# Two places where side work is put into longer runs: the experts' gathers and scatters, and the second attention's products with values

## The chip, the cores and the metric

The kernel runs on one core of a Trainium2 chip. The metric is device time in microseconds (us), lower is better: the time of one execution on that core, as the median of several runs. One more execution was profiled; all rows below are from it. The engines are TensorE (PE, and PEld for its weight loads), VectorE (DVE), ScalarE (ACT), GpSimd (POOL) and SyncE (SP), which issues most of the DMAs.

## The reference

The input is one sequence of 512 tokens with 1024 features. Three blocks are chained: two transformer layers (attention, then a squared-ReLU MLP) and a third layer whose MLP is a mixture of experts. All is in float32. Two parts matter here.

The second layer's attention has 16 heads in 2 groups and three branches for each head, added with gates:

```
s_c = q . kc          # 31 compressed keys
o_c = softmax(s_c) . vc
o_s = softmax(masked q . k_sel) . v_sel      # selected blocks
o_w = softmax(masked q . k_win) . v_win      # window
out = g0 * o_c + g1 * o_s + g2 * o_w
```

With 512 tokens the number of kept blocks and the window both cover the whole sequence, so the second and the third branch are plain causal attention with their own keys and values.

The mixture of experts routes each of the 512 tokens to 2 of 32 experts; expert e computes

```
ys = (silu(xb @ w1[e]) * (xb @ w3[e])) @ w2[e]      # 1024 -> 512 -> 1024
out[token] += gate * ys
```

The weights of all experts are 32 x 3 x 1024 x 512 floats, 201 MB.

## The kernel before

The kernel runs the layers one after another; in time: first layer's attention, its MLP, second layer's attention, its MLP, third layer's attention, router and experts. The order of each engine's instructions is written out by hand: a function that is called issues its instructions there and then, and each engine works its own queue in order. Matrices of the dense layers are split in a high and a low part (`whi`, `wlo`), so that fp32r matmuls keep float32's accuracy.

**Second layer's attention** (`layer_1`). `pair_items(f)` (line 1350) makes the work for two heads, f from 0 to 7. It is a list of 10 items for a `Pipeline` (line 543). An item is one softmax over up to 512 columns (`softmax_item`, line 574): scores on PE (`qk`), maximum on DVE, exponential on ACT, scaling with the gate on POOL (line 606), transposes on PE (`T`, line 611), a copy of the transposed tile to SBUF (`hi`, line 614, into a tile of tag `PT`, 8 buffers), and products with the values on PE (`pv`, which calls `take`). The table `SM1` (line 28) says how many steps after the item's first step each part is issued: scores 0, maximum 1, exponential 2, scaling 3, transposes 5, copy 6, values 7, out 8. Each step of the pipeline issues the due parts of all items that are under way. The value products are done for two heads side by side by `two_columns` (line 624): each uses half of the columns of TensorE's array, with 64 columns of weights, which the profile prints as "128*64". Query blocks i of 128 rows are grouped as (3), (2 and 0), and (1). For (3) and for (2, 0) the branches b = 0 and 1 have items of their own, two (one for each head, a = 0 and 1), and `take` for a branch is called in the second of them: `both_pv` for the blocks of that branch. For block 1 both branches share two items. The first `take` also calls `started(f)`, the product with the compressed values (`pcT`), into the same PSUM bank. So there are five bursts of value products for each f.

**Experts** (`experts`, line 1905). Experts are taken in 16 pairs r, up to 64 tokens each. `first(r)` does the products with w1 and w3 (8 steps k), `second(r)` those with w2 (4 steps k). A step is one `product` (line 1989): it takes two weight tiles of 128 x 1024 floats, one of each expert of the pair, as the moving operand, and the two experts' tokens use the two halves of the array's columns ("128*64" again). Two instructions stand in the trace for each of its four float32 matmuls. The weight tiles stream through a ring of 24 SBUF tiles (`RING`, `load`); `two()` takes a pair of tiles and issues the loads of the pair 24 places further on, on SP's queue, which wait until the ring's tiles are free.

Beside the products, tokens must be brought to the experts and back by matmuls with one-hot matrices that use the whole array. `gather(q)` (line 1955) serves two pairs of experts, 34 units of work; `scatter([r-1, r])` (line 2052) adds the results of two pairs to x, 16 units of two matmuls each, a bank of four matmuls being added to x on DVE (line 2063). Both are generators in a list `work`; `fill(n)` (line 1935) issues the next n units. `FILL1` and `FILL2` (lines 82, 83) say after which step k of `first` and `second` how many units are issued: 16 in each `first`, in three places, 11 in each `second`, in two. `drain` issues what is left of one kind. `spread(r)` (line 2045) makes the one-hot matrix `ot` of the scatter with one matmul (32 rows of weights, "32*128") from `pick` and `posT` and a comparison on DVE; it stands inside `second`, after step 2. `turn(r)` transposes the hidden layer between the two products.

The loop (line 2084) goes `first(r)`, `second(r-1)`, `turn(r)`. Behind the last product, `second(15)`, what is left of the scatters is drained, and the output leaves block by block.

Of the kernel before, what the change touches and what calls it, by code (L numbers as in the profile page):

```python
# [9 lines left out]
F32 = mybir.dt.float32  # L10
F32R = mybir.dt.float32r
I32 = mybir.dt.int32
AF = mybir.ActivationFunctionType
# [5 lines left out]
S = 512  # L19
# [24 lines left out]
NE, CAP = 32, 64  # L44
# [34 lines left out]

FTILES = {'fraw': 8, 'fsum': 2, 'S2': 1, 'parth': 3, 'partl': 3, 'fwhi': 3, 'fwlo': 3}  # L80

FILL1 = {2: 5, 5: 5, 7: 6}
FILL2 = {1: 5, 3: 6}


@with_exitstack
def tile_kernel(ctx: ExitStack, tc: tile.TileContext, I, out, stage=None, start=None):
    nc = tc.nc
# [10 lines left out]
    def ps(rows=128, cols=512):  # L99
        t = psum.tile([128, 512], F32, tag="ps", name="ps")  # L100
        return t[:rows, :cols]
# [17 lines left out]
    ident = cst[:, K_ID:K_ID + 128]  # L119
# [504 lines left out]
    def two_columns(o, at, of, start=False, stop=False):  # L624

        for c in range(2):
            nc.tensor.matmul(o[c * 64:c * 64 + 64, at], *of(c), start=start, stop=stop, skip_group_check=True,  # L627
                             tile_position=(0, c * 64))
# [6 lines left out]
    def lazy(f):  # L635
        box = []

        def get():
            if not box:
                box.append(f())  # L640
            return box[0]
        return get
# [439 lines left out]
    def layer_1():  # L1082
# [244 lines left out]
        def started(f):  # L1327
            o = ps()
            two_columns(o, slice(0, S), lambda a: (vcs[f // 4][:, f % 2 * 2 + a], pcT[:, f // 2, :]), start=True)
            return o  # L1330

        def ended(f, o):
            nc.scalar.activation(oh[:, f], o, AF.Copy)
            nc.vector.tensor_tensor(ol[:, f], o, oh[:, f], ALU.subtract)
# [9 lines left out]
        def both_pv(i, at, b, p, o, g):  # L1344

            for j in range(i + 1):
                two_columns(o, slice(i * 128, i * 128 + 128),
                          lambda c: (vsw[:, j, b * 2 + g], p[c]()[:, at + j * 128:at + j * 128 + 128]), stop=j == i)

        def pair_items(f):  # L1350
            o = lazy(lambda: started(f))
            new = lambda: att.tile([128, S], F32, tag="PT", name="PT", bufs=8)
            out = []
            nothing = lambda: None

            def items(segs, take, use=nothing):
                p = [lazy(new), lazy(new)]
                for a in range(2):
                    out.append(softmax_item(SM1, segs(a), qk, lambda n, i: cmask[:, 384 - i * 128:],
                                            lambda n, i: gate[:, i, n // 2 * 3 + 1 + n % 2:n // 2 * 3 + 2 + n % 2],  # L1360
                                            p[a], (lambda: take(p)) if a else nothing, use if a else nothing, a))
            for part in ((3,), (2, 0)):
                for b in range(2):
                    def take(p, part=part, b=b):
                        for i, at in zip(part, (0, 384)):
                            both_pv(i, at, b, p, o(), f // 4)
                    items(lambda a, b=b, part=part: [(4 * f + 2 * a + b, i) for i in part], take)

            def last(p):
                for b in range(2):  # L1370
                    both_pv(1, 256 * b, b, p, o(), f // 4)
            items(lambda a: [(4 * f + 2 * a, 1), (4 * f + 2 * a + 1, 1)], last, lambda: ended(f, o()))
            return out

        items = [cmp_item(0, 0), cmp_item(0, 2)]
        for f in range(8):
            if f == 3:
                items += [cmp_item(1, 0), cmp_item(1, 2)]
            items += pair_items(f)
# [380 lines left out]


    def moe():
        posT = att.tile([NE, S], F32R, name="posT")
        ghl = att.tile([128, NT, NE, 2], F32R, name="ghl")
        with phase("experts") as sub:
            experts(sub, posT, ghl)
        with phase("overflow") as sub:
            overflow(sub)
# [136 lines left out]
    def experts(sub, posT, ghl):  # L1905
# [3 lines left out]
        work, picks, ot = [], [], {}  # L1909
        pairs = NE // 2  # L1910
        last = pairs - 1
# [17 lines left out]
        def two():  # L1929
            i = used[0]  # L1930
            used[0] += 2
            load(i + len(RING))
            return tiles[i:i + 2]

        def fill(n):
            while n and work:
                if next(work[0], work) is work:
                    work.pop(0)
                else:
                    n -= 1  # L1940

        def drain(name):
            while any(w.__name__ == name for w in work):
                fill(1)
# [44 lines left out]
        def product(p, k, nk, xs, w):  # L1989

            for n in range(2):
                for b in range(2):
                    nc.tensor.matmul(p[n][half(b)], xs[:, half(b)], w[b][:, n * 512:n * 512 + 512],  # L1993
                                     start=k == 0, stop=k == nk - 1)

        def first(r):
            p = ps(), ps()
            for k in range(KD):
                product(p, k, KD, xt[r // 2][k][:, r % 2 * 128:r % 2 * 128 + 128], two())
                if k == KD - 1:  # L2000
                    s = sub.tile([128, S], F32, tag="silu", name="silu", bufs=1)
                    hs[r] = sub.tile([128, S], F32, tag="hs", name="hs", bufs=2)
                    nc.scalar.activation(s, p[0], AF.Silu)  # L2003
                    nc.vector.scalar_tensor_tensor(hs[r], s, gcol[r], p[1], ALU.mult, ALU.mult)
                fill(FILL1.get(k, 0))

        def turn(r):
            p = ps()
# [6 lines left out]
        def second(r):  # L2015
            if r % 2 == 0:
                drain("scatter")
            h = hid.pop(r)
            p = ps(), ps()
            ys[r] = [sub.tile([128, D], F32R, tag="y" + s, name="y" + s, bufs=2) for s in "hl"]  # L2020
            for k in range(4):
                product(p, k, 4, h[:, k], two())
                if k == 3:
                    for n in range(2):
                        nn = slice(n * 512, n * 512 + 512)
                        split_evac(ys[r][0][:, nn], ys[r][1][:, nn], p[n])
                if k == 2:
                    spread(r)
                if r < last:
                    fill(FILL2.get(k, 0))  # L2030
            if r >= last - 1:
                work.append(scatter([r]))
            elif r % 2:
                work.append(scatter([r - 1, r]))
            if r == last:
                drain("scatter")

        def picking(r):

            pick = sub.tile([NE, 128], F32R, tag="pick", name="pick", bufs=2)  # L2040
            nc.gpsimd.tensor_copy(pick.rearrange("p (e s) -> p e s", e=2),  # L2041
                                  ident[0:NE, 2 * r:2 * r + 2][:, :, None].to_broadcast([NE, 2, CAP]))
            picks.append(pick)

        def spread(r):

            p = ps()
            nc.tensor.matmul(p, picks[r], posT, start=True, stop=True)  # L2048
            ot[r] = sub.tile([128, S], F32R, tag="ot", name="ot", bufs=3)
            nc.vector.tensor_scalar(ot[r], p, iota[:, 64:65], None, op0=ALU.is_equal)  # L2050

        def scatter(rs):

            for t in range(NT):
                for n in range(2):
                    p = ps()
                    nn = slice(n * 512, n * 512 + 512)
                    for j, r in enumerate(rs):
                        for a in range(2):
                            nc.tensor.matmul(p, ot[r][:, t * 128:(t + 1) * 128], ys[r][a][:, nn],  # L2060
                                             start=j == 0 and a == 0, stop=j == len(rs) - 1 and a == 1)
                        yield
                    nc.vector.tensor_tensor(x[:, t, nn], p, x[:, t, nn], ALU.add)
                if rs[-1] == last:
                    finish(t)
# [1 line left out]

        make_o(0)
        sub.tile([128, S], F32R, tag="ot", name="ot", bufs=3)
        sub.tile([NE, 128], F32R, tag="pick", name="pick", bufs=2)  # L2070
        sub.tile([128, 8], F32, tag="gs", name="gs", bufs=2)
        sub.tile([128, PAD], F32, name="pad")
        for c in "ab":
# [1 line left out]
        load(len(RING))  # L2075
        nc.scalar.activation(ghl[:, :, :, 0], gates, AF.Copy)
        nc.gpsimd.tensor_tensor(ghl[:, :, :, 1], gates, ghl[:, :, :, 0], ALU.subtract)
        p = ps(NE)
        for t in range(NT):
            nc.tensor.transpose(p[:, t * 128:(t + 1) * 128], posm[:, t], ident)  # L2080
        nc.scalar.activation(posT, p, AF.Copy)
        work.append(gather(0))
        drain("gather")
        for r in range(pairs + 1):
# [211 lines left out]
```

## Time and profile before

| | |
|---|---|
| runs before, us | 2154.09, 2155.61, 2158.60 (median 2155.61) |
| the profiled execution, us | 2152.04 |
| its span, first to last instruction, us | 2150.2 |
| TensorE busy, share of the span | 2064.6 us, 96% |
| VectorE, ScalarE, GpSimd busy | 52%, 37%, 20% |
| moved from HBM | 324.49 MB |
| second layer's attention, steady part | about 784 to 917 us |
| experts' products | 1650 to 2129 us |

Times of rows are microseconds from the span's start. Matmuls are pipelined, so one matmul's duration is longer than the step from its start to the next one's; steps are what count. Weight loads (PEld) run ahead of the matmuls where they can.

### The profile page before, as it was taken

How to read it: one execution, taken by the hardware profiler on the slowest of the kernel's cores; microseconds unless marked ns; L12 is line 12 of the kernel's file. 1: busy time of each engine (PE TensorE's matmuls, PEld its weight loads, DVE VectorE, ACT ScalarE, POOL GpSimd, SP SyncE). 2: the span in 40 equal slices, each digit the busy share in tenths (PEclk: the TensorE clock that was granted, in tenths of full speed). 3: DMA queues.
4: the chain of work that ended last, by engine and by line, in shares of the span. 5: the costliest groups of instructions: out<-in, count | busy, mean ns of one | idle time of the engine just before them, and what ended most of it. 6: DMA issues, size and time to landing. Idle time of an engine off the chain costs nothing.

```text
span 2150.2 us, 28736 instructions
## 1 busy us (share of the span) xinstructions
PE 2064.6 (96%) x10871; PEld 1503.5 (70%) x10871; DVE 1111.4 (52%) x2273; ACT 798.0 (37%) x1530; POOL 421.8 (20%) x548
## 2 busy tenths in 40 slices
PE   7999999999999999999999999989998999999997
PEld 6786688888888777888888887767766444444443
DVE  5486544768764567634768766443724132222223
ACT  4525533434443357733434444453632101010000
POOL 2344420000002355620000002553352000000000
PEclk9999999999999999999999999999998999999998
DMA  4231025233232210024242231302045999999994
GB/s 136 70 98 30 21 89 166 72 125 108 69 94 90 61 39 2 2 89 138 75 143 85 89 98 58 108 20 88 11 162 209 418 417 408 409 416 403 406 405 185
DMA packets 118829, 328.58 MB, mean 153 GB/s; under 512 B 10604, under 2 KB 12716, under 8 KB 118688
## 3 DMA queue, kind: packets, MB, share of 16 engines
q1 hardware_dynamic: 115888, 318.87, 40.9%
q0 software_dynamic: 2800, 7.84, 1.2%
q8 instruction: 87, 1.43, 0.3%
q14 instruction: 54, 0.44, 0.1%
HBM read 324.49 MB, written 2.11 MB: 152 GB/s over the span
## 4 chain that ended last, share of the span: by engine, by line
PE 57%; DVE 4%; ACT 2%; POOL 1%; issue 1%; DMA 0%; DVEq 0%; POOLq 0%; ACTq 0%
PE ps L1993 16%; PE ps L404 10%; PE ps L347 8%; PE ps L696 5%; PE ps L1964 3%; PE ps L2060 2%; PE ps L627 2%; PE ps L611 2%; PE ps L1341 2%; POOL wlo L280 1%; PE ps L1710 0%; ACT P L1598 0%; PE ps L2011 0%; DVE room L469 0%; PE ps L1712 0%
## 5 line engine op out<-in xcount | busy, mean ns | idle before, releaser
L267 ACT ACTIVATE whi<-raw 128x1024 fp32r<-128x1024 f32 (+2 forms) x162 | 168.4, 1042 | 384.4 <-PE ps L404 155.0
L280 POOL TENSOR_TENSOR wlo<-raw,whi 128x512 fp32r<-128x512 f32 (+1 forms) x132 | 168.8, 1301 | 381.4 <-ACT whi L267 368.3
L282 DVE TENSOR_TENSOR wlo<-raw,whi 128x1024 fp32r<-128x1024 f32 (+2 forms) x96 | 118.3, 1233 | 225.1 <-ACT whi L267 224.9
L1993 PE MATMUL ps<-ew,xt 128*64 128x512 f32 x1024 | 229.9, 597 | 0.0
L404 PE MATMUL ps<-oTl,whi 128*128 128x512 f32 (+2 forms) x576 | 211.4, 371 | 1.4 <-DVE oTl L311 1.4
L404 PE MATMUL ps<-oTh,whi 128*128 128x512 f32 (+2 forms) x576 | 211.6, 371 | 0.5 <-ACT oTh L310 0.5
L404 PE MATMUL ps<-oTh,wlo 128*128 128x512 f32 (+2 forms) x576 | 166.7, 370 | 0.0
L1993 PEld LDWEIGHTS ps<-ew,xt 128*64 128x64 f32 x1024 | 69.4, 137 | 128.2 <-issue 111.3
L347 PE MATMUL ps<-whi,uTh 128*128 128x512 f32 (+2 forms) x384 | 151.3, 395 | 2.3 <-ACT uTh L310 2.3
L347 PE MATMUL ps<-whi,uTl 128*128 128x512 f32 (+2 forms) x384 | 147.7, 386 | 2.3 <-DVE uTl L311 2.2
L404 PEld LDWEIGHTS ps<-oTl,whi 128*128 128x128 f32 x576 | 108.5, 188 | 20.9 <-DVE oTl L311 2.1
L404 PEld LDWEIGHTS ps<-oTh,whi 128*128 128x128 f32 x576 | 108.5, 188 | 19.6 <-ACT oTh L310 1.0
L347 PE MATMUL ps<-wlo,uTh 128*128 128x512 f32 (+2 forms) x384 | 117.5, 386 | 4.2 <-POOL wlo L280 4.2
L1993 PE MATMUL ps<-ew,hid 128*64 128x512 f32 x512 | 118.4, 600 | 0.7 <-ACT hid L2013 0.7
L404 PEld LDWEIGHTS ps<-oTh,wlo 128*128 128x128 f32 x576 | 104.8, 188 | 18.7
L647 DVE TENSOR_TENSOR x<-ps,x 128x512 f32<-128x512 f32 x124 | 82.0, 684 | 65.0 <-PE ps L347 38.0
L598 ACT ACTIVATE P<-P,nm 128x384 f32<-128x384 f32 (+2 forms) x192 | 106.3, 557 | 22.3 <-DVE nm L591 19.1
L445 POOL DMA_DIRECT2D room<-gains x5 | 2.8, 566 | 566.3 <-DVE fwlo L289 566.3
L591 DVE CUSTOM_DVE_ANT_0 P<-ps,cst 128x128 f32<-128x128 f32 (+3 forms) x168 | 74.9, 473 | 37.9 <-POOL P L606 18.6
L2041 POOL CAST pick<-cst 32x128 fp32r<-32x128 f32 x16 | 4.9, 307 | 443.5 <-PE ps L2048 443.5
L2003 ACT ACTIVATE silu<-ps 128x512 f32<-128x512 f32 x16 | 9.6, 597 | 212.8 <-PE ps L1993 212.8
L347 PEld LDWEIGHTS ps<-wlo,uTh 128*128 128x128 f32 x384 | 72.5, 192 | 20.3 <-POOL wlo L280 6.9
(548 smaller groups left out, 4544.7 us busy)
## 6 DMA issues: line engine op xcount, KB each, us to landing
ew<-w SPq DMA_DIRECT2D x384, 512.0 KB, 9.4
raw<-mlp_w SPq DMA_DIRECT2D x80, 512.0 KB, 3.7
fraw<-mlp_w SPq DMA_DIRECT2D x48, 512.0 KB, 5.8
raw<-w_in SPq DMA_DIRECT2D x24, 512.0 KB, 3.8
raw<-ab_w_in SPq DMA_DIRECT2D x20, 512.0 KB, 3.6
raw<-c_w_in SPq DMA_DIRECT2D x12, 512.0 KB, 3.6
raw<-ab_w_out SPq DMA_DIRECT2D x8, 512.0 KB, 3.9
raw<-c_w_out SPq DMA_DIRECT2D x8, 512.0 KB, 3.7
```

Of the source, the lines that this page charges most:

```text
L267: nc.scalar.activation(hi[:, :w], raw[:, :w], AF.Copy)
L280: nc.gpsimd.tensor_tensor(lo[:, h], raws[r][:, h], hi[:, h], ALU.subtract)
L282: nc.vector.tensor_tensor(lo[:, :w], raws[r][:, :w], hi[:, :w], ALU.subtract)
L347: nc.tensor.matmul(p, a[:, tt], w[:, k], start=u == 0 and n == 0, stop=u == nk - 2 and n == 5)
L404: nc.tensor.matmul(p[:, tt], w[:, k, ff], b[:, u + k, tt], start=start and n == 0, stop=u == nk - 2 and n == 5, **kw)
L591: nc.vector.tensor_tensor_reduce(st["p"][:, a], st["s"][c], in1(h, i), 1.0, 3e38, ALU.add, ALU.min, st["nm"][:, c:c + 1])
L598: nc.scalar.activation(p, p, AF.Exp, scale=-1.0, bias=st["nm"][:, c:c + 1], accum_out=st["sm"][:, c:c + 1])
L611: nc.tensor.transpose(st["t"][:, j:j + 128], st["p"][:, j:j + 128], ident)
L647: nc.vector.tensor_tensor(xs, p, xs, ALU.add)
L696: nc.tensor.matmul(acc[b][t], p[:, 2 * h + k, tt], v[:, k], start=begins and h == 0 and m == 0, stop=m == 5, skip_group_check=True)
L1964: nc.tensor.matmul(v, htok[a][:, t, c * 128:(c + 1) * 128], oo[q][:, t], start=t == 0 and a == 0, stop=t == NT - 1 and a == 1)
L1993: nc.tensor.matmul(p[n][half(b)], xs[:, half(b)], w[b][:, n * 512:n * 512 + 512], start=k == 0, stop=k == nk - 1)
```

## The change

In the second layer's attention the items of both branches keep their order, but `take` is called once for a group of blocks, in the last of its four items, and does `both_pv` for both branches. In the experts, `fill` is called once at the end of `first` (16 units) and once at the end of `second` (11 units), and `spread` moves from after step 2 to the end of `second`. `pick` and `posT` get 128 partitions instead of 32, with zeros in the new ones. The last two pairs' scatters become one, like the others.

```diff
-FILL1 = {2: 5, 5: 5, 7: 6}
-FILL2 = {1: 5, 3: 6}
+FILL1, FILL2 = 16, 11
...
-            def items(segs, take, use=nothing):
-                p = [lazy(new), lazy(new)]
+            def items(segs, p, take, use=nothing):
                 for a in range(2):
                     out.append(softmax_item(SM1, segs(a), qk, lambda n, i: cmask[:, 384 - i * 128:],
                                             lambda n, i: gate[:, i, n // 2 * 3 + 1 + n % 2:n // 2 * 3 + 2 + n % 2],
-                                            p[a], (lambda: take(p)) if a else nothing, use if a else nothing, a))
+                                            p[a], take if a else nothing, use if a else nothing, a))
             for part in ((3,), (2, 0)):
+                p = [[lazy(new), lazy(new)] for _ in range(2)]
+
+                def take(p=p, part=part):
+                    for i, at in zip(part, (0, 384)):
+                        for b in range(2):
+                            both_pv(i, at, b, p[b], o(), f // 4)
                 for b in range(2):
-                    def take(p, part=part, b=b):
-                        for i, at in zip(part, (0, 384)):
-                            both_pv(i, at, b, p, o(), f // 4)
-                    items(lambda a, b=b, part=part: [(4 * f + 2 * a + b, i) for i in part], take)
+                    items(lambda a, b=b, part=part: [(4 * f + 2 * a + b, i) for i in part], p[b], take if b else nothing)
...
-        posT = att.tile([NE, S], F32R, name="posT")
+        posT = att.tile([128, S], F32R, name="posT")
...
                     nc.vector.scalar_tensor_tensor(hs[r], s, gcol[r], p[1], ALU.mult, ALU.mult)
-                fill(FILL1.get(k, 0))
+            fill(FILL1)
...
-                if k == 2:
-                    spread(r)
-                if r < last:
-                    fill(FILL2.get(k, 0))
-            if r >= last - 1:
-                work.append(scatter([r]))
-            elif r % 2:
+            spread(r)
+            if r < last:
+                fill(FILL2)
+            if r % 2:
                 work.append(scatter([r - 1, r]))
...
-            pick = sub.tile([NE, 128], F32R, tag="pick", name="pick", bufs=2)
+            pick = sub.tile([128, 128], F32R, tag="pick", name="pick", bufs=2)
...
+        nc.gpsimd.memset(posT.bitcast(F32), 0.0)
...
-        nc.scalar.activation(posT, p, AF.Copy)
+        nc.scalar.activation(posT[0:NE], p, AF.Copy)
```

## Rows read from the trace of the kernel before

**Rows 1.** Stretches: us, busy of PE, PEld, DVE, ACT, POOL, clock, DMA.

```profile
1650.00:2129.00 479.00, 478.31 (x2346) 214.29 (x2345) 111.08 (x224) 46.78 (x79) 3.97 (x14) 1.00 0.98 395
1700.00:1750.00 50.00, 50.00 (x255) 24.45 (x252) 10.48 (x29) 4.18 (x7) 0.28 (x1) 1.00 1.03 418
1850.00:1900.00 50.00, 50.00 (x242) 22.40 (x241) 11.90 (x25) 4.13 (x7) 0.28 (x1) 1.00 1.01 406
```

**Rows 2.** Waits, 1650 to 2128: us, times, longest; weight loads only.

```profile
PEld ps L1964 <- issue: 34.1, 42, 0.8
...
PEld ps L2048 <- issue: 13.0, 16, 0.8
...
PEld ps L2011 <- issue: 7.3, 9, 0.8
PEld ps L1977 <- issue: 5.7, 7, 0.8
PEld ps L2060 <- ACT silu L2003: 4.9, 6, 0.8
PEld ps L2060 <- issue: 2.4, 3, 0.8
```

**Rows 3.** Timeline of PE: start, us, line, tiles, form, count.

```profile
2068.49 13.95 PE L1993 MATMUL ps<-ew,xt 128*64 128x512 f32 x64
2082.27 5.32 PE L1993 MATMUL ps<-ew,hid 128*64 128x512 f32 x24
...
2087.95 1.94 PE L1993 MATMUL ps<-ew,hid 128*64 128x512 f32 x8
...
2098.20 5.37 PE L1993 MATMUL ps<-ew,xt 128*64 128x512 f32 x24
...
2103.84 0.40 PE L2060 MATMUL ps<-yl,ot 128*128 128x512 f32 x1
...
2105.70 0.40 PE L2060 MATMUL ps<-yl,ot 128*128 128x512 f32 x1
2106.03 3.65 PE L1993 MATMUL ps<-ew,xt 128*64 128x512 f32 x16
```

**Rows 4.** Waits of SP's DMA queue, 1700 to 1750 us.

```profile
SPq L1927 <- DMA ew<-w: 33.9, 39, 1.5
```

**Rows 5.** Waits of SP's DMA queue, 1850 to 1900 us.

```profile
SPq L1927 <- PE ps L1993: 28.3, 19, 6.6
```

**Rows 6.** Tile ew, all 384 loads: issue to landing.

```profile
DMA to landing us min/median/max: 3.4/9.4/10.6
```

**Rows 7.** Timeline of SP's queue from 1650 us.

```profile
1652.06 47.52 SPq L1927 DMA_DIRECT2D ew<-w  x42
```

**Rows 8.** Timeline of DVE from 2129 us.

```profile
2130.46 9.65 DVE L2063 TENSOR_TENSOR x<-ps,x 128x512 f32<-128x512 f32 x16
```

**Rows 9.** Groups of instructions from 1560 us: count, busy us, mean ns, idle before.

```profile
L2050 DVE TENSOR_SCALAR ot<-ps,cst 128x512 fp32r<-128x512 f32 x16 | 12.0, 751 | 93.2 <-PE ps L2048 93.2
```

**Rows 10.** Timeline of PE in the second attention's steady part.

```profile
865.23 0.48 PE L1341 MATMUL ps<-kst01h,qst 128*128 128x512 f32 x1
...
865.78 0.60 PE L611 MATMUL ps<-cst,P 128*128 128x128 f32 x4
866.14 0.48 PE L1341 MATMUL ps<-kst11h,qst 128*128 128x512 f32 x1
...
866.78 1.09 PE L627 MATMUL ps<-PT,vsw 128*64 128x128 f32 x16
```

**Rows 11.** Timeline at the start of the second attention's pipeline.

```profile
781.90 1.97 PE L627 MATMUL ps<-PT,vsw 128*64 128x128 f32 x14 [3.62 <-DVE PT L614]
782.03 4.30 POOL L606 TENSOR_SCALAR P<-P,sm,gate 128x384 f32<-128x384 f32 x8 [2.35 <-DVE sm L603]
```

**Rows 12.** Stretches of the second attention; columns as in Rows 1.

```profile
780.00:800.00 20.00, 18.10 (x156) 15.68 (x157) 14.51 (x57) 14.66 (x46) 10.39 (x18) 0.83 0.08 28
...
850.00:870.00 20.00, 20.00 (x195) 16.55 (x195) 14.35 (x58) 15.48 (x47) 11.87 (x20) 1.00 0.01 2
```

More of the change, by code (lines that the diff above doesn't have):

```diff
@@ L1360, in items, with last @@
                                             lambda n, i: gate[:, i, n // 2 * 3 + 1 + n % 2:n // 2 * 3 + 2 + n % 2],
-                                            p[a], (lambda: take(p)) if a else nothing, use if a else nothing, a))
+                                            p[a], take if a else nothing, use if a else nothing, a))
             for part in ((3,), (2, 0)):
-                for b in range(2):
-                    def take(p, part=part, b=b):
-                        for i, at in zip(part, (0, 384)):
-                            both_pv(i, at, b, p, o(), f // 4)
-                    items(lambda a, b=b, part=part: [(4 * f + 2 * a + b, i) for i in part], take)
-            def last(p):
+                p = [[lazy(new), lazy(new)] for _ in range(2)]
[3 more added lines that the diff above has]
+                            both_pv(i, at, b, p[b], o(), f // 4)
+                for b in range(2):
+                    items(lambda a, b=b, part=part: [(4 * f + 2 * a + b, i) for i in part], p[b], take if b else nothing)
+            p = [lazy(new), lazy(new)]
+            def last(p=p):
                 for b in range(2):
                     both_pv(1, 256 * b, b, p, o(), f // 4)
-            items(lambda a: [(4 * f + 2 * a, 1), (4 * f + 2 * a + 1, 1)], last, lambda: ended(f, o()))
+            items(lambda a: [(4 * f + 2 * a, 1), (4 * f + 2 * a + 1, 1)], p, last, lambda: ended(f, o()))
             return out
@@ L2038, in picking @@
         def picking(r):
-            pick = sub.tile([NE, 128], F32R, tag="pick", name="pick", bufs=2)
+            pick = sub.tile([128, 128], F32R, tag="pick", name="pick", bufs=2)
             nc.gpsimd.tensor_copy(pick.rearrange("p (e s) -> p e s", e=2),
-                                  ident[0:NE, 2 * r:2 * r + 2][:, :, None].to_broadcast([NE, 2, CAP]))
+                                  ident[:, 2 * r:2 * r + 2][:, :, None].to_broadcast([128, 2, CAP]))
             picks.append(pick)
@@ L2069, in experts @@
         sub.tile([128, S], F32R, tag="ot", name="ot", bufs=3)
-        sub.tile([NE, 128], F32R, tag="pick", name="pick", bufs=2)
+        sub.tile([128, 128], F32R, tag="pick", name="pick", bufs=2)
         sub.tile([128, 8], F32, tag="gs", name="gs", bufs=2)
```

## The prediction

> **What bounds the kernel now.** The profiled execution took 2152.0 us around a span of 2150.2 us; the median of the runs is 2155.6 us, 3.6 us more. I read first the busy times by stretch. From 1650 to 2129 us, the experts' stage, TensorE is busy 478.3 of 479 us, and the core's DMA engines show a share of 0.98, over 1 in the stretches inside it [rows 1]: two resources are full together, and a gain on one is limited by the other. So two clocks must be kept.
>
> TensorE's clock: in the stage it never waits for a result. What it loses stands in the waits of the weight loads. Each time a run of the experts' products (64 columns of weights, "128*64") is left for another kind of matmul, the next weight load comes some 0.8 us late instead of being prefetched: 42 + 16 + 9 + 7 + 6 + 3 = 83 times [rows 2]. The price of one such departure and return is read from the timeline [rows 3]. Eight products without a break took 2082.27 - 2068.49 = 13.78 us, 1.72 each. Three products and 10 scatter matmuls took 2106.03 - 2098.20 = 7.83 us; the scatter's own step is (2105.70 - 2103.84)/8 = 0.23 us, so 7.83 - 3 x 1.72 - 10 x 0.23 = 0.36. For three products with one `spread` between them: 2087.95 - 2082.27 - 5.17 - 0.23 = 0.28. I take 0.33.
>
> The stream's clock: 384 tiles of 0.524 MB go through a ring of 24. Where SyncE waits only for earlier transfers (33.9 of 50 us) [rows 4] the stream makes 418 GB/s, 1.254 us a tile; where it waits mostly for TensorE to free a tile (28.3 of 50 us) [rows 5] it makes 406 [rows 1]. So the stream is at its own limit in some stretches, and held back only a little in others.
>
> **Experts, TensorE alone.** `fill(16)` after `first` and `spread` + `fill(11)` + `turn` after `second` leave 2 departures per pair of experts. Pair 14 has nothing to fill after `first`, and pair 15's `spread` joins the scatter behind the last product, so inside the products 15 + 15 = 30 remain of 83. Saved: 53 x 0.33 = 17.5 us, and 0.2 for the `spread` that leaves: 17.7. No matmul is added. The longer runs are covered: 16 units of scatter are eight banks of four matmuls, 0.92 us a bank, against an addition of 0.60 us each [rows 8], so VectorE keeps up.
>
> **Experts, the stream.** The stretch most exposed is pair 14 and the first product of pair 15, where no fill is left between the products: TensorE asks for 24 tiles in 12 x 1.72 = 20.6 us, the stream needs 30. Where does each stand at the last product of `first(15)`? Before, it started at 2106.03 + 1.72 = 2107.75 [rows 3]. By then 79 of the 83 departures lie behind it before and 28 after: 51 x 0.33 = 16.8 us earlier; and the 20 scatter matmuls that stood in front of it now stand behind it: 4.6 more. TensorE would be there at 2086.3. That product needs the 368th tile. The first 24 are loaded early; the 25th is issued at 1652.06 [rows 7], unchanged, as it waits for the first product, and lands 3.4 us later at best [rows 6], at 1655.5. 343 more tiles at 418 GB/s end at 1655.5 + 430.2 = 2085.7: no wait. At the 406 of the other stretch (1.291 us) they end at 2098.3: a wait of 12. With TensorE freeing tiles earlier, SyncE should wait for transfers nearly always, so I lean to 418, but slower spots that belong to the stream itself will stay: I take 413 GB/s, 1.270 us, 2090.9, a wait of 4.6. Behind that point come 16 units of scatter (7.4 us) in which the stream gets ahead again, and the last 16 tiles don't bind. Sum: -17.7 + 4.6 = -13.1 us (bounds -17.7 and -5.7).
>
> The Trainium skill bears on this end: DMA: Bandwidth & Descriptors (section Bandwidth) gives 425 GB/s as measured for one core alone on a large load, and 358 as a core's share of HBM. By 425 TensorE would never wait and the stage would give the whole 17.7 (rival A); by 358 this stage could not exist, since 201 MB would take 562 us. The trace's 418 agrees with the first figure and contradicts the second here.
>
> **Experts, edges.** Before, pair 14's scatter ran while the last results were evacuated, and 16 additions ended at 2130.46 + 9.65 = 2140.1 [rows 8]. Now pair 15's `spread` is compared on VectorE (0.75 us [rows 9]) behind those evacuations: ready at 2130.46 + 0.75 = 2131.2 on the same time axis. The first two scatter matmuls go before it, TensorE then waits some 1.5 us, 30 matmuls at 0.23 end about 2138.1, the last one's tail and an addition make it 2139.2: -0.9 (bounds +1 and -1.5), as eight additions instead of 16 no longer set the pace. The memory set of `posT` on GpSimd delays ScalarE's copy of it, which is first needed behind the second pair's `first`; queued behind it on ScalarE is only the gather's evacuation. `pick` grows only in partitions. Nothing (bounds 0 and +0.5).
>
> **Second layer's attention.** In its steady part TensorE also runs without a gap, 20.00 of 20 us [rows 12]. From a step's scores to its values it is 866.78 - 866.14 = 0.64 us, from scores to the next transposes, without values, 865.78 - 865.23 = 0.55 [rows 10]: the entry alone costs 0.09. With the return a burst of values costs between that and the 0.33 above; I take 0.28, near the price that holds both ways. Bursts per pair of heads go from 5 to 3, over 8 pairs 16 fewer: -4.5 us (bounds -5.3 and -1.4). Against it: at the start of the pipeline TensorE stands 3.6 us for the first values' copy [rows 11], and meanwhile, and at a lowered clock, does the first burst (14 matmuls in 1.97 us). Now that burst moves two steps back, TensorE stands at the transposes instead, which wait for GpSimd's scaling starting at 782.03 [rows 11], and the opening product with the compressed values and both bursts come after the stall: I charge +2 (bounds 0 and +4). Longer bursts in one step and none in three could let ScalarE fall behind; it is busy 15.48 of 20 us there [rows 12] and no row shows TensorE late on it: nothing, but +2 as an upper bound. Value tiles live two steps longer, 4 or 5 of 8 buffers: no wait. Sum -2.5 (bounds -5 and +4).
>
> **Sum.** -13.1 - 0.9 - 2.5 = -16.5: 2135.5 in the profiled execution's terms, 2155.6 - 16.5 = 2139.1 against the median. Forecast 2139 us.
>
> **Rivals.**
> A, the stream keeps pace: at 418 GB/s or better TensorE never waits: -17.7 - 0.9 - 2.5 = -21.1, or -23 if the attention gains all: 2134. For it: the 418 in undisturbed stretches. Against: even there TensorE's pace of consumption was lower than it will be, and the margin at the critical product is 0.6 us.
> B, the stream falls back: long runs without a product (23 units, over 9 us, every second pair) free no tile; if the ring fills, transfers stop and restart, and the mean falls to 406: -5.7 - 0.9 - 2.5 = -9.1, 2146.5; at 400, 1.311 us a tile, the wait is 18.8 and the stage gains nothing: with the rest -2.3, 2153, no change.
> C, slower: TensorE's clock. Granted 1.00 throughout the stage [rows 1], it fell to a mean of 0.83 in the 20 us around the attention's 3.6 us stall [rows 12], between the 1.2 and 2.4 GHz levels. If TensorE, waiting for tiles in pairs 14 and 15, drops to 1.2 GHz, a product takes 3.44 us instead of the stream's 2.54: 20 products x 0.9 = 18 us, and the gain is gone (about 2157); if the lower level lasts to the last product, 8 x 1.72 + 7.4 = 21 more, 2178. [...] Against it: TensorE stays two thirds busy.
> D, it doesn't do what it says: the cost sits in each return to products with fresh weights, not in the change of kind, or `spread` at 128 rows costs what it saves: no change, 2153 to 2156.
>
> **How the numbers follow.** Forecast (the stream catches TensorE in pair 14) 0.55; A 0.2; B 0.15, a fifth of it within no change; C 0.05; D 0.05. The range takes A and most of B: 2131 to 2150. A measurement of this kernel tells about 0.2%, 4.3 us, from no change. Faster by more: 0.55 + 0.2 + 0.12 + a little = 0.88; same 0.07; slower 0.05.
>
> **What would show it.** Departures from products fall from 83 to about 30, each at the same price. A run of 12 products between two bursts should appear; TensorE's waits on weight tiles first show in pair 14 or 15, and DMA there reads 413 to 418 GB/s. If no wait on tiles shows and the last product ends 17 us earlier, A is right. If GB/s stays at 406 with waits from pair 8 on, B. The granted clock below 1.00 before the tail would show C. In the attention, three value bursts per pair of heads instead of five, and a longer first stall. A stage of products that is not at least 8 us shorter makes the account of the departures wrong.

## The result, and the profile after

The changed kernel takes 2139.69 us (median of 4 runs, 2138.48 to 2140.22) against 2156.52 us of the kernel before in the same runs: a ratio of 0.9922, 95% interval 0.9904 to 0.9939. The forecast was 2139. Its profiled execution took 2139.59 us around a span of 2137.8, which is 12.4 us less than the span before, while the medians differ by 16.8. So the two profiles are compared stage by stage, not by their ends. Line numbers of the changed kernel are one less or two more than before (L1995 the products, L2047 `spread`, L2059 the scatter, L1966 the gather).

First the experts' stage. These are stretches of the profile after, with the columns of [rows 1]; the second and third answer to the last of [rows 1].

```profile
1650.00:2112.00 462.00, 460.41 (x2350) 220.06 (x2351) 110.89 (x225) 46.78 (x79) 4.15 (x14) 1.00 1.01 409
1850.00:1900.00 50.00, 50.00 (x253) 23.85 (x251) 12.04 (x24) 3.59 (x6) 0.30 (x1) 1.00 1.03 418
2050.00:2100.00 50.00, 49.09 (x213) 18.30 (x210) 8.01 (x12) 4.78 (x8) 0.59 (x2) 1.00 1.03 418
```

Where the stream made 406 GB/s before, it now makes 418, and TensorE's granted clock stays at 1.00. The waits of SP's DMA queue from 1850 to 1900 us, against [rows 5], say why: it hardly waits for TensorE to free a tile (2.1 us, before 28.3), but for earlier transfers.

```profile
SPq L1929 <- DMA ew<-w: 34.5, 40, 1.1
SPq L1929 <- PE ps L1995: 2.1, 6, 0.4
```

The matmuls of the products, with first and last start: the stage, from the first product's first matmul to the last one's last, takes 2118.3 - 1654.1 = 464.2 us. Before it took 478.5.

```profile
L1995 PE MATMUL ps<-ew,xt x1024: 592/592/644, 1654.1 to 2095.2; 128*64 128x512 f32 x171
L1995 PE MATMUL ps<-ew,hid x512: 592/592/643, 1690.1 to 2118.3; 128*64 128x512 f32 x171
```

The waits of the weight loads from 1654 to 2118 us, against [rows 2]. The 0.8 us entries that were 42, 16, 9, 7, 6 and 3 are now 15, 13, 1 and 1. The entry for weight tiles was there before as well, in a line that [rows 2] leave out, with 54 waits of at most 0.4 us; that line stands first. What is new is its longest wait: six of the 53 are over 0.45 us, all in `first(15)`, from 2081.3 to 2093.8 us.

```profile
PEld ps L1993 <- DMA ew<-w: 15.6, 54, 0.4
```

```profile
PEld ps L1995 <- DMA ew<-w: 18.7, 53, 1.1
PEld ps L2047 <- issue: 12.2, 15, 0.8
PEld ps L1966 <- issue: 10.5, 13, 0.8
...
PEld ps L1966 <- PE ps L1995: 0.8, 1, 0.8
PEld ps L2059 <- ACT silu L2005: 0.8, 1, 0.8
```

Most of those 18.7 us lie beside running matmuls. What they cost stands in the timeline of TensorE at the end of the stage: `first(14)` and `second(13)` run into one another (64 + 32 instructions, two per float32 matmul), and in `first(15)`, from its fourth product on, the products come only every 2.5 us instead of every 1.72.

```profile
2055.57 13.95 PE L1995 MATMUL ps<-ew,xt 128*64 128x512 f32 x64
2069.36 7.04 PE L1995 MATMUL ps<-ew,hid 128*64 128x512 f32 x32
2076.33 0.51 PE L2047 MATMUL ps<-posT,pick 128*128 128x512 f32 x1
2076.67 0.60 PE L2013 MATMUL ps<-cst,hs 128*128 128x128 f32 x4
2077.20 6.46 PE L1995 MATMUL ps<-ew,xt 128*64 128x512 f32 x26
2083.84 2.32 PE L1995 MATMUL ps<-ew,xt 128*64 128x512 f32 x8 [0.18 <-DMA ew<-w]
...
2093.82 1.93 PE L1995 MATMUL ps<-ew,xt 128*64 128x512 f32 x6 [0.18 <-DMA ew<-w]
2095.69 0.50 PE L2059 MATMUL ps<-yh,ot 128*128 128x512 f32 x1
```

From its first matmul to the scatter behind it `first(15)` takes 2095.69 - 2077.20 = 18.49 us.

The end of the kernel, VectorE's timeline (against [rows 8]): the additions no longer follow one another without a gap, each waits 0.2 us for TensorE's four matmuls.

```profile
2120.18 0.74 DVE L2049 TENSOR_SCALAR ot<-ps,cst 128x512 fp32r<-128x512 f32 x1
2121.81 0.69 DVE L2062 TENSOR_TENSOR x<-ps,x 128x512 f32<-128x512 f32 x1 [0.89 <-PE ps L2059]
...
2128.19 0.69 DVE L2062 TENSOR_TENSOR x<-ps,x 128x512 f32<-128x512 f32 x1 [0.21 <-PE ps L2059]
```

From the last product's last matmul to the end it is 2137.8 - 2118.3 = 19.5 us, before 21.6.

The second attention, TensorE's timeline at the start of the pipeline (against [rows 11]): it now stands 5.68 us at the transposes, and the opening product and one burst of 32 come behind.

```profile
780.01 0.28 PE L1340 MATMUL ps<-kst10l,qst 128*128 128x256 f32 x1
785.97 1.12 PE L610 MATMUL ps<-cst,P 128*128 128x128 f32 x4 [5.68 <-POOL P L605]
...
789.57 1.35 PE L626 MATMUL ps<-pcT,vcs 128*64 128x512 f32 x4
790.75 1.91 PE L626 MATMUL ps<-PT,vsw 128*64 128x128 f32 x32
```

### The profile page after: what moved, and what is told of

Same layout as the page of the kernel before. It is cut to its first block, busy times and chain, and to the rows that moved or that the text cites. A ratio compares the mean times of both kernels' runs of the same rounds, so it can differ in the third digit from the quotient of the medians.

```text
span 2137.8 us, 28715 instructions
## 1 busy us (share of the span) xinstructions
PE 2050.0 (96%) x10871; PEld 1510.1 (71%) x10871; DVE 1106.7 (52%) x2265; ACT 796.6 (37%) x1530; POOL 423.0 (20%) x549
## 4 chain that ended last, share of the span: by engine, by line
PE 53%; DVE 4%; DMA 3%; ACT 2%; POOL 2%; issue 1%; POOLq 0%; DVEq 0%; SPq 0%; ACTq 0%
PE ps L1995 13%; PE ps L403 10%; PE ps L346 9%; PE ps L695 5%; DMA ew<-w 3%; PE ps L1966 3%; PE ps L2059 2%; PE ps L626 2%; PE ps L610 2%; PE ps L1340 2%; POOL wlo L279 1%; PE ps L1712 0%; ACT P L1600 0%; PE ps L1271 0%; PE ps L1714 0%
## 5 line engine op out<-in xcount | busy, mean ns | idle before, releaser
L1995 PE MATMUL ps<-ew,xt 128*64 128x512 f32 x1024 | 227.0, 594 | 0.9 <-DMA ew<-w 0.9
L1995 PEld LDWEIGHTS ps<-ew,xt 128*64 128x64 f32 x1024 | 72.9, 137 | 143.4 <-issue 125.9
L403 PEld LDWEIGHTS ps<-oTh,whi 128*128 128x128 f32 x576 | 108.5, 188 | 19.6 <-ACT oTh L309 1.0
L2006 DVE SCALAR_TENSOR_TENSOR hs<-silu,gs,ps 128x512 f32<-128x512 f32 x16 | 12.0, 748 | 213.0 <-PE ps L1995 213.0
L1995 PE MATMUL ps<-ew,hid 128*64 128x512 f32 x512 | 113.3, 595 | 0.7 <-ACT hid L2015 0.7
L2040 POOL CAST pick<-cst 128x128 fp32r<-128x128 f32 x16 | 4.7, 299 | 427.0 <-PE ps L2047 427.0
L309 ACT ACTIVATE yh<-ps 128x512 fp32r<-128x512 f32 x32 | 19.1, 598 | 184.9 <-PE ps L1995 184.9
```

The source lines that it names most:

```text
L403: nc.tensor.matmul(p[:, tt], w[:, k, ff], b[:, u + k, tt], start=start and n == 0, stop=u == nk - 2 and n == 5, **kw)
```

## The experiments

Each kernel is told by its median, the experts' stage (first to last product's matmul), the tail (from there to the span's end) and the attention's stretch: from the matmul that stood last before the first product with values before (`kst10l` at 776.8 us there) to the last product with values. Up to that matmul TensorE's instructions are the same in all these kernels. Times are us. Medians compare only within a set of runs: beside the two halves and the second profiles the kernel before took 2155.58, beside the next four kernels 2154.32, beside the last three 2158.16.

| kernel | median (profiled execution alone in brackets) | stage | tail | attention's stretch |
|---|---|---|---|---|
| before, first profile | 2156.52 | 478.5 | 21.6 | 140.5 |
| before, second profile | (2157.44) | 478.5 | 21.6 | 140.7 |
| after, first profile | 2139.69 | 464.2 | 19.5 | 138.4 |
| after, second profile | 2138.13 | 463.7 | 19.7 | 138.1 |
| after, third profile | 2137.87 | 464.1 | 19.8 | 138.7 |
| experts' part alone | 2137.70 | 464.6 | 19.7 | 140.6 |
| attention's part alone | 2155.19 | 478.5 | 21.6 | 138.2 |
| first pair of heads as before | (2137.51) | 464.3 | 19.6 | 137.8 |
| fills two by two | 2169.70 | 497.8 | 19.6 | 138.5 |
| spread on 32 rows | (2136.30) | 464.5 | 19.9 | 138.6 |
| no scatters of 14 pairs | (2136.89) | 460.9 | 20.3 | 138.2 |
| scatters 12 and 13 apart | 2133.75 | 460.7 | 19.6 | 138.6 |
| the same, attention as before | 2136.31 | 461.2 | 19.8 | 140.5 |

**The two halves.** The kernel before with the experts' hunks of the diff alone:

> The kernel before with only the experts' part of the change. My theory (the departures carry the gain, the stream takes a piece back): 31 runs of products instead of 84, a wait on weight tiles of some 4 us in pair 14's and 15's products, stage 14 us and tail 2 us shorter: 2139 to 2143 us. Rival 'the attention matters as much': then this alone would stay above 2147. Rival 'the parts depend on each other' (a later start of the stage gives the stream a lead): a stage gain that differs from the whole change's 14.3 us by over 2 us.

Measured: 2137.70 us, ratio 0.9919 (0.9903 to 0.9935), 17.5 us faster (14.0 to 20.9), 1.3 us under the expected range. 31 runs of products, stage 13.9 and tail 1.9 us shorter. The gain is here. With the attention's hunk alone:

> The kernel before with only the attention's part. My theory: 16 bursts of values fewer give 4.5 us back, the stall at the start of the pipeline grows from 3.6 to 5.7 us and takes 2 us and some clock with it: 1 to 3 us faster than before, 2153 to 2155. Rival 'the start eats it all': within 0.5 us of before. Rival 'the stretches at the lower clock that the profile after shows outside the changed code belong to the attention's change': slower than before by 1 to 4 us.

Measured: 2155.19 us, ratio 0.9996 (0.9985 to 1.0006), so between 3.2 us faster and 1.3 slower. Its stretch is 2.3 us shorter, but the time doesn't show it: the interval holds both 2.3 us and nothing.

**The same kernels again.**

> The changed kernel once more, on the same chip as the two halves. My theory: 2138 to 2141, the gains of the two halves add up to it within 2 us, and the stretches at the lower clock outside the changed code fall elsewhere in its profile than in the first. Rival 'the change moves those stretches': the same stretches (745 to 750, 1420 to 1425, 1515 to 1525 us) at the lower clock again.

Measured: 2138.13 us, ratio 0.9918 (0.9903 to 0.9933). The time is as expected, and the gains of the two halves (17.9 and 0.4) add up to its 17.5 within 2 us. The low stretches at 745 and 1420 us were there again, the one at 1515 to 1525 us wasn't; so of the clock neither theory held whole. The kernel before once more:

> The kernel before, unchanged, for a second profile. My theory: 2152 to 2159 us, and stretches at the lower clock in the first and third layer that the first profile doesn't have, which make its experts start 1 to 5 us later than 1650.1 without anything changed. Rival: the same stretches as in the first profile and the same start within 0.5 us; then the later start in the changed kernel belongs to the change.

Measured: 2157.44 us; its first product starts at 1655.6 us, 5.5 later than in its first profile, a little more than expected, and 1.5 later than in the changed kernel's, while stage and tail agree to 0.01 us. So the start of the experts moves by itself. Two rows of windows (columns as above) show one place where the clock differs: this profile of the kernel before with the clock at 1.00, and a kernel with the attention of before (the last of the table) with 0.66.

```profile
745.00:750.00 5.00, 5.00 (x32) 4.30 (x31) 1.71 (x3) 2.55 (x4) 1.04 (x1) 1.00 0.00 0
```

```profile
745.00:750.00 5.00, 4.50 (x20) 3.92 (x21) 1.76 (x3) 0.60 (x1) 0.00 (x0) 0.66 0.00 0
```

**The start of the attention.** In `pair_items`, f = 0 alone keeps a burst for each branch:

```diff
+                    def early(b=b, p=p, part=part):
+                        for i, at in zip(part, (0, 384)):
+                            both_pv(i, at, b, p[b], o(), f // 4)
-                    items(..., p[b], take if b else nothing)
+                    items(..., p[b], early if f == 0 else take if b else nothing)
```

> The changed kernel, with the values of the first pair of heads taken branch by branch as before. From the last scores before the pipeline's first values to the last product with values it took 140.5 and 140.7 us without the attention's change and 138.4 and 138.1 with it. My theory: the longer stall at the start (5.7 against 3.6 us) is given back, two bursts at 0.28 come again: 136.5 to 137. Rival 'the stall only moves to the next late step': 138 or more, with a wait of the same 2 us somewhere between 785 and 800.

Measured: 137.8, between the two, in a single profile. The stall is back to 3.62 us, and no other of 2 us comes in its place, yet only some 0.5 us are gained:

```profile
779.36 0.38 PE L626 MATMUL ps<-PT,vsw 128*64 128x128 f32 x2
783.36 1.97 PE L626 MATMUL ps<-PT,vsw 128*64 128x128 f32 x14 [3.62 <-DVE PT L613]
785.26 1.12 PE L610 MATMUL ps<-cst,P 128*128 128x128 f32 x4
```

The transposes behind it start 785.26 - 778.25 = 7.0 us after the `kst10l` matmul at 778.25, and in the changed kernel 785.97 - 780.01 = 6.0: the longer stall is for the most part the same wait with less work in front of it.

**The price of a departure.** The 16 units behind `first`, issued by twos:

```diff
-            fill(FILL1)
+                fill(2)          # inside the loop over k
```

> The changed kernel with the 16 units behind each first product issued two at a time behind each of its eight steps: the same matmuls, 7 departures more in each of 14 pairs, about 98. My theory (each departure costs about 0.33 us whatever its length): 98 x 0.33 = 32 us of TensorE more, less the 4 us that TensorE then no longer waits for weight tiles: 2164 to 2170. Rival 'short visits are cheaper' (0.2): 2154 to 2158. Rival D, no price for a departure: 2139.

Measured: 2169.70 us, ratio 1.0068 (1.0049 to 1.0086). 136 runs of products instead of 31, and no wait on the stream that costs. One round is read in the timeline, from product to product:

```profile
1764.99 1.94 PE L1995 MATMUL ps<-ew,xt 128*64 128x512 f32 x8
1766.86 0.39 PE L1966 MATMUL ps<-o,h2h 128*128 128x256 f32 x1
1767.08 0.28 PE L1966 MATMUL ps<-o,h2l 128*128 128x256 f32 x1
1767.20 0.28 PE L1966 MATMUL ps<-o,h2h 128*128 128x256 f32 x1
1767.32 0.28 PE L1966 MATMUL ps<-o,h2l 128*128 128x256 f32 x1
1767.53 1.94 PE L1995 MATMUL ps<-ew,xt 128*64 128x512 f32 x8
```

2.54 us, less 1.72 for the product and 4 x 0.12 for the gather's matmuls, leaves 0.34. By the stage: 33.6 us more, and the wait of 4.6 (below) gone, over 105 more departures: 0.36. A visit of half a microsecond of work pays the same entry and return as one of 7 us. This is the clearest of the runs, and it puts rival D away: the same matmuls in more pieces take 33.6 us longer.

**The one-hot's matmul at 32 rows again**, `pick` and `posT` on 32 partitions:

> The changed kernel with pick and posT on 32 partitions as before, so that the one-hot's matmul is again one with 32 rows of weights among matmuls with 128. My theory: the grouping carries the gain; other time in the stage (125.8 us of gathers, scatters, turns) grows by at most 0.1 a time, 0 to 1.5 us. Rival: the 32 rows are a departure of their own, 0.28 x 15 = 4 us more of other time.

Measured: the stage as long as in the changed kernel (464.5 us), but other time 128.7 instead of 125.8 us: 2.9 us over 15 times, 0.19 each. Neither was right; and none of it reaches the end, as TensorE waits that much less for tiles. As long as TensorE runs into the stream, the 128 rows are worth nothing.

**Who ends the stage.**

```diff
-            if r % 2:
+            if r == last:
                 work.append(scatter([r - 1, r]))
```

> The changed kernel without the scatters of the first 14 pairs (7 x 32 matmuls of 0.23 us, 51 us of TensorE, and their additions are left out; their results don't reach x). My theory: the stage is at the stream's own pace, so only what TensorE holds back goes: first to last product 455 to 460 us against 464.2, waits on weight tiles in nearly all pairs, 418 GB/s, and the granted clock stays at 1.00. Rival 'TensorE sets the stage': 464 - 51 = 413 to 425 us. Rival C: with the many waits of 0.8 us the clock falls below 1.00 in the stage.

Measured: 460.9 us, 0.9 above the expected range. 51 us of TensorE's work leave, and the stage gets 3.3 us shorter: it stands on the stream. Its last product's last matmul starts at 2114.87 us, 1.38 us behind the landing of the last tile (2113.49). The windows show TensorE with gaps, the transfers at 418 GB/s, the clock at 1.00, which puts rival C away as well:

```profile
1850.00:1900.00 50.00, 48.86 (x232) 21.57 (x231) 9.24 (x20) 5.86 (x10) 0.59 (x2) 1.00 1.03 418
2050.00:2100.00 50.00, 46.91 (x165) 13.71 (x164) 3.53 (x5) 2.98 (x5) 0.29 (x1) 1.00 1.03 418
```

The 353 landings from the 31st tile to the last come every 1.261 us on average and every 1.248 in the median, in the changed kernel as here: some landings 0.2 to 0.9 us late belong to the stream, whoever uses it. The Trainium skill, DMA: Bandwidth & Descriptors (section Bandwidth), gives 425 GB/s for one core alone; no stretch of 50 us in these kernels goes above 419, even here, where TensorE waits for tiles.

**A version that beats both.** Pair 12's scatter is issued apart, so that its 8 units stand between `first(14)` and `second(13)`:

```diff
-            if r % 2:
+            if r == last - 3 or r == last - 2:
+                work.append(scatter([r]))
+            elif r % 2:
                 work.append(scatter([r - 1, r]))
```

> The changed kernel with the scatters of pairs 12 and 13 apart, so that pair 12's 8 units (3.7 us) stand between the products of first(14) and second(13), where TensorE ran into the stream, and the run of 12 products is parted. My theory: the wait on weight tiles in first(15) falls from 4.2 to about 0.5 us; then the last tiles bind, which land 461 us or less after the first product, so the stage goes from 464.2 to 461 to 462: 2135 to 2137 us. Rival 'the wait comes back whole at the last products': 464, 2138 to 2140.

Measured: 2133.75 us, ratio 0.9889 (0.9864 to 0.9915), stage 460.7, 3.4 us shorter than the 464.1 of the changed kernel beside it (below); faster than expected by 1 us. By the medians alone (2133.75 against 2137.87, with overlapping intervals) that the version is faster would only be likely; the stage, which repeats to some 0.5 us, shows it. The products of `first(15)` now run without the pause:

```profile
2052.56 13.96 PE L1995 MATMUL ps<-ew,xt 128*64 128x512 f32 x64
2066.45 0.50 PE L2061 MATMUL ps<-yh,ot 128*128 128x512 f32 x1
...
2078.18 14.15 PE L1995 MATMUL ps<-ew,xt 128*64 128x512 f32 x64
2092.26 0.50 PE L2061 MATMUL ps<-yh,ot 128*128 128x512 f32 x1
```

`first(14)` with its departure is 13.89 us here, so the 18.49 of the changed kernel's `first(15)` hold a wait of 4.6 us. The last matmul of the products now starts 1.38 us behind the last tile (2110.35 and 2111.73 us), as in the kernel without scatters, where in the changed kernel it started 4.5 us behind (2113.76 and 2118.3): here the stream ends the stage. The same with the attention of before:

> The same scatters apart with the attention of before. If the attention's change gives 2.3 us in its stretch and nothing elsewhere, this is about 2 us slower than the kernel above; if its gain is lost elsewhere, the same within 1 us. In its profile the stretch from the last scores before the first values to the last product with values takes 140.5 us.

Measured: 2136.31 us, ratio 0.9904 (0.9878 to 0.9929), 2.6 slower in the median; the intervals overlap, so it only points to the first theory. The changed kernel beside them:

> The changed kernel once more, beside the two above. My theory: 2138 to 2140, stage 463.7 to 464.6 us, and whether TensorE's clock falls at 745 us is chance, since seven profiles with the new attention have it four times and every instruction up to there is that of the kernel before. Rival: the fall belongs to the new attention after all and is there again here and in the first of these kernels.

Measured: 2137.87 us, ratio 0.9914 (0.9888 to 0.9939), stage 464.1. The clock stayed at 1.00 at 745 us, here and in the first of these kernels. Of 13 profiles 5 have the fall there: 4 of 9 with the new attention, and 1 of 4 with the old one (shown above). The last is what the rival can't have.

## Why the prediction was right, step by step

**Departures.** Predicted 83 to about 30 at 0.33 us; the profile has 30. Stage 14.3 us shorter, with a wait of 4.6 in it that wasn't there: TensorE alone gave 18.9 against 17.7 predicted. Less the 0.2 of the `spread` that left, it is 18.7/53 = 0.35 for each, near the larger of the two prices of [rows 3] (0.36 and 0.28), between which I had taken 0.33. The 128 rows of `spread` have a part in it: with 32 rows the other time is 2.9 us longer (above), which would leave 15.8/53 = 0.30.

**The stream.** Predicted 4.6 us of wait at the last products of `first(15)`, measured 4.6. The mechanism is as told; that the two agree to a tenth is luck, since, counted from the first product, the last tile of `first(15)` landed 1.1 us earlier than predicted (439.7 us against 440.8) and TensorE without its wait would have been there 1.1 us earlier too (435.1 against 436.2). The 368th tile landed at 2093.78 us, the 25th at 1659.59: 343 tiles in 434.2 us, 1.266 each or 414 GB/s; I had taken 1.270. That the spots of the stream itself stay, which put 413 in place of 418, was the step that decided between the forecast and rival A: A needed every tile in 1.254 us. B is out, since the stretches show 418. C is out as well: with products only every 2.5 us in `first(15)` the granted clock stayed at 1.00. The sign that waits on weight tiles first show in pair 14 or 15 holds for the waits that hold up the products; short ones of the weight loads stand all through the stage, before as after.

**Tail.** Predicted -0.9, measured -2.1 (-1.8 to -2.1 in three profiles). The additions did what was said: the last one ends 10.6 us behind the last product's matmul, before 11.5. Missing was what comes behind: the four output transfers are issued 1.82 us apart instead of 1.19, and the last one lands in 3.5 us instead of 4.6.

**Attention.** Predicted -2.5, measured -1.8 to -2.6 in its stretch (two profiles of before, three of after); a good sum of two wrong terms. Counted from the last product with values of one pair of heads to that of the next, each of the last four pairs gets 0.60 us shorter (16.06 to 15.46), 0.30 a burst, against 0.28. But only there: in the two first profiles the first pair is 0.7 us longer (22.30 to 22.97; 0.2 to 1.0 over all profiles), the second gets nothing, the third 0.4, the fourth 0.1. The +2 stood for the start alone; it was some 1.3 (0.7, and two bursts saved in vain), and 1.4 us went in the next three pairs. For the second and the third the trace shows the cause; for the fourth it is open. In the third pair TensorE waits 1.3 us for GpSimd's scaling behind the compressed scores, where before it stood 1.0 us one step later for their own softmax. In the second pair the weight loads of the transposes wait for GpSimd's scaling (line 605), and two steps of transposes take 0.73 and 0.53 us instead of 0.41 and 0.35:

```profile
813.51 0.20 PEld L610 LDWEIGHTS ps<-cst,P 128*128 128x128 f32 x2 [0.37 <-POOL P L605]
814.05 0.20 PEld L610 LDWEIGHTS ps<-cst,P 128*128 128x128 f32 x2 [0.34 <-POOL P L605]
815.13 0.20 PEld L610 LDWEIGHTS ps<-cst,P 128*128 128x128 f32 x2 [0.19 <-POOL P L605]
```

That is 0.5 us of the 0.6; before, the weight loads there wait 0.17 us for GpSimd. Those bursts were taken off an engine that waits for GpSimd anyway.

**From the profile to the median.** The forecast added a difference to the median of before, and that was right: the profiled execution of before was 3.6 us below the median of the three runs known then and 4.5 below that of the four here (2156.52), that of after 0.1. Taken from the two profiles alone the gain would be 12.4. The rest lies ahead of the experts: the first product starts 4.0 us later than in the profile before, although the attention's stretch is 2.1 us shorter, so 6.2 us were lost in stretches whose instructions are the same. In those stretches the clock stood at its lower level for 58 us instead of 44; whether that is the whole of the 6.2 us isn't shown. The forecast's closeness to the median is in part luck: by the profiles stage, tail and attention together gave 14.3 + 2.1 + 2.1 = 18.5 us, 2 more than the 16.5 forecast, while the medians of three sets of runs differ by 16.8, 17.5 and 20.3.

## What to carry to other kernels

Where matmuls of two forms alternate, count the departures, not the matmuls: each cost 0.34 to 0.36 us here, with half a microsecond of work in the visit as with 7 (0.28 for the single matmul of [rows 3]). Then set the second clock beside the first: when an engine gets 19 us faster over a stream that has 18 to give (478.5 to 460.7), look for the point where the consumer first catches the stream, and put work that is already due just ahead of it (3.4 us here). And merge for an engine only where it waits for nothing: bursts saved while TensorE waits for GpSimd came back as waits.

## What the runs showed of the hardware that wasn't expected

The clock falls in different places in executions with the same instructions. After the waits of 0.55 and 1.37 us at 743 to 745 us the granted clock fell to 0.50 in 5 of 13 profiles and stayed at 1.00 in 8; a fall there moved all that follows by 1.6 us, and with others in the third layer the first product started anywhere from 1648.4 to 1655.6 us (some 2 us of it by the attention's change). The page TensorE: Matmul & The Clock Gate of the Trainium skill (section Part 1: The HAM clock gate) says that the number of matmuls at the low clock at a kernel's start varies from run to run of one kernel; these rows show the like in its middle. The stage itself repeats to 0.01 us where TensorE alone sets it (478.48 in two profiles of before) and to 0.5 where the stream does (463.7 to 464.2).
